# Time-mixing stage: pa as one tile of two banks, D in X's bank, Y's state products beside X's, groups issued in a fixed order

## The chip, the cores and the metric

The kernel runs on one core of a Trainium2 chip. The metric is the device time of one execution in microseconds (us), the median of the runs. In the profile PE is the matmul engine and PEld its weight loads, DVE the vector engine, ACT the scalar engine, POOL the general engine, and SP issues the transfers (DMA).

## The reference

Two layers over 1024 latent and 256 context tokens of width 1024. Each layer norms its input, projects it, runs three mixers side by side and merges them. The change lies in the first mixer, a recurrence over tokens in two directions, with 8 heads of 64 x 64 state:

```python
def rwkv7_scan(r, v, kk, decay, k_dir, akk, state0, reverse):
    """S_t = S_{t-1} (diag(w_t) - kk_t^T (a_t kk_t)) + v_t^T k_t ;  y_t = S_t r_t."""
    def step(s, inp):
        r_t, v_t, kk_t, w_t, k_t, akk_t = inp
        s_kk = jnp.einsum('bhvk,bhk->bhv', s, kk_t)
        s = s * w_t[:, :, None, :] - s_kk[..., None] * akk_t[:, :, None, :] + v_t[..., None] * k_t[:, :, None, :]
        return s, jnp.einsum('bhvk,bhk->bhv', s, r_t)
    s_fin, ys = lax.scan(step, state0, xs, reverse=reverse)
```

The context's recurrence runs first and hands its last state to the latent tokens. In the last layer only the latent tokens' y is used. Everything is float32.

## The kernel before

**The stage.** `rwkv_stage` works through 20 chunks of 64 tokens, both directions d and all heads at once. Heads come as 4 pairs `pr`; `p` is the member of a pair, and it says which half of the 128 partitions its operands lie in (0 to 63 or 64 to 127). So a group of products over d, pr and p is 16 calls, and each call on fp32 operands is two matmul instructions in the profile, 32 in all. The transposes (L617) are one each.

**prep(c)**, which runs ahead, loads bkT, kr and uv (L588, L589, L594), multiplies them into pa (L604), masks pa on DVE into mb (L607), copies mb's diagonal blocks to dg on ACT (L612), transposes bkT on PE into pt (L617) and copies that to bk on ACT (L618). Then DVE transposes dg to at (L624) and inverts small triangular blocks step by step (P and R, L640 to L657); their inverse is tt (L659). bkT, dg, at, R and P have one buffer each, bk two, mb and kr three.

**chain(c)** carries the state S. X gathers products of mb and uv (L667) and of kr and S (L670). Twice, ACT copies X to x1 (L675), PE multiplies by tt into U (L679), and DVE (p = 0) and ACT (p = 1) copy U to uv (L684); between the two, X gets one more product (L689). D is the product of bk and uv (L693), from which DVE makes the next S (L696, L697). Y, where the chunk has an output (all 20 chunks in layer 0, 16 in layer 1), gathers S with kr (L703) and uv with mb (L706); ACT copies it to yst (L709, L710).

**PSUM.** It has 8 banks. The pool `pre` has two slots of one bank, used in turn for pa of p = 0, pa of p = 1 and pt; `chn` has a bank each for X, U, D and Y; `pj`, outside the stage, has two for projections.

**Order.** The program is written chunk after chunk, but a scheduler sets the order of instructions on each engine when the kernel is built: whatever is ready first by its own reckoning goes first, and earlier code has priority. Each engine then runs its instructions in that order, and so does SP its transfers. Between the stage's products the scheduler places projections that don't depend on it (pjt, L150: `z_stage`, at the end `g_stage`), three matmuls of up to 512 columns for each block of weights. `tc.issue_after(ins)` makes what is traced in its block stand behind `ins` on that engine; it asks for the order alone, not for a wait.

Of the kernel before, what the change touches and what calls it, by code (L numbers as in the profile page):

```python
# [8 lines left out]
F32 = mybir.dt.float32  # L9
# [3 lines left out]
ALU = mybir.AluOpType  # L13
AX = mybir.AxisListType
PSUM = bass.MemoryType.PSUM
# [22 lines left out]
def tile_backbone(ctx: ExitStack, tc: tile.TileContext, xT_in, cond_in, w_mod, vecs, w_in, d_up, a_up,  # L38
                  qkg, lqk, w_br, w_out, consts, rope, out):
    nc = tc.nc  # L40
    te, ve, se, gp, dma = nc.tensor, nc.vector, nc.scalar, nc.gpsimd, nc.sync

    def pool(name, bufs=1, space=None, es=ctx):
        kw = {} if space is None else {"space": space}
        return es.enter_context(tc.tile_pool(name=name, bufs=bufs, **kw))
# [19 lines left out]
    mask = cst[:, C_MASK:C_MASK + 128]  # L65
# [68 lines left out]
    def run_late(ins=None):  # L134
        due = []
        for e in late[:]:
            e[0] -= 1
            if ins is None or e[0] <= 0:
                due.append(e[1])
                late.remove(e)  # L140
        for f in due:
            with tc.issue_after(ins) if ins is not None else ExitStack():
                f()

    def mm3(ps, terms):
        n = 3 * len(terms)
# [426 lines left out]
    def rwkv_stage(l):  # L573
        full = l < NL - 1
        es = ExitStack()
        rp = pool("rp", es=es)
        pre = pool("pre", bufs=2, space=PSUM, es=es)
        chn = pool("chn", bufs=1, space=PSUM, es=es)
        units = [(d, pr, p) for d in range(2) for pr in range(4) for p in range(2)]
        f8 = lambda a: a.rearrange("p d a v -> p (d a) v")  # L580

        def prep(c):
# [11 lines left out]
                    dma.dma_start(out=uv[64 * p:64 * p + 64, d, p].rearrange("t a v -> t (a v)"),  # L594
                                  in_=v_dr[l][d][row:row + 64, 256 * p:256 * p + 256])
            mb = rp.tile([128, 2, 2, 4, 128], F32, tag="mb", name="mb", bufs=3)
            mk = mask[:, 0:ny].unsqueeze(1).to_broadcast([128, 4, ny])
            for d in range(2):

                pas = [pre.tile([128, 4, 128], F32, tag="pre", name="pa") for p in range(2)]  # L600
                for pr in range(4):
                    for p in range(2):
                        s = slice(64 * p, 64 * p + 64)
                        te.matmul(out=pas[p][:, pr, 0:ny], lhsT=bkT[s, 4 * d + pr, :], rhs=kr[s, 4 * d + pr, 0:ny],  # L604
                                  start=True, stop=True)
                for p in range(2):
                    ve.tensor_tensor(out=mb[:, d, p, :, 0:ny], in0=pas[p][:, :, 0:ny], in1=mk, op=ALU.mult)  # L607
            dg = rp.tile([128, 2, 4, 32], F32, tag="dg", name="dg", bufs=1)
            for p in range(2):
                for q in range(2):  # L610
# [1 line left out]
                    se.copy(out=dg[s], in_=mb[s, :, p, :, 32 * q:32 * q + 32])  # L612
            bk = rp.tile([128, 2, 4, 128], F32, tag="bk", name="bk", bufs=2)
            for d in range(2):
                pt = pre.tile([128, 4, 128], F32, tag="pre", name="pt")
                for pr in range(4):
                    te.transpose(out=pt[:, pr, :], in_=bkT[:, 4 * d + pr, :], identity=ident)  # L617
                se.copy(out=bk[:, d], in_=pt)  # L618
# [42 lines left out]

        def chain(c, st, S, yst):
            y, kr, mb, bk, uv, tt = st
            half = [slice(64 * p, 64 * p + 64) for p in range(2)]
            X = chn.tile([128, 2, 4, 64], F32, tag="X", name="X")
            for d, pr, p in units:
                te.matmul(out=X[half[1 - p], d, pr, :], lhsT=mb[half[p], d, p, pr, 0:64], rhs=uv[half[p], d, p, pr, :],  # L667
                          start=(d == 0 and pr == 0), stop=False, skip_group_check=True)
            for d, pr, p in units:
                te.matmul(out=X[half[1 - p], d, pr, :], lhsT=kr[half[p], 4 * d + pr, 0:64], rhs=S[half[p], d, pr, :],  # L670
                          start=False, stop=False, skip_group_check=True)
            U = chn.tile([128, 2, 4, 64], F32, tag="U", name="U")
            for q in range(2):
                x1 = rp.tile([128, 2, 4, 64], F32, tag="xs", name="xs", bufs=1)
                se.copy(out=x1, in_=X)  # L675
                for d, pr, p in units:
                    b0 = 64 * (1 - p)
                    s = slice(b0 + 32 * q, b0 + 32 * q + 32)
                    te.matmul(out=U[s, d, pr, :], lhsT=tt[s, 4 * d + pr, :], rhs=x1[s, d, pr, :], start=True,  # L679
                              stop=True, skip_group_check=True)  # L680
                for p, cp in ((0, ve.tensor_copy), (1, se.copy)):
                    b0 = 64 * (1 - p)
                    s = slice(b0 + 32 * q, b0 + 32 * q + 32)
                    cp(out=uv[s, :, p], in_=U[s])  # L684
                if q == 0:
                    for d, pr, p in units:
                        b0 = 64 * (1 - p)
                        s = slice(b0, b0 + 32)
                        te.matmul(out=X[b0 + 32:b0 + 64, d, pr, :], lhsT=mb[s, d, p, pr, 32:64],  # L689
                                  rhs=uv[s, d, p, pr, :], start=False, stop=True, skip_group_check=True)  # L690
            D = chn.tile([128, 2, 4, 64], F32, tag="D", name="D")
            for d, pr, p in units:
                te.matmul(out=D[half[p], d, pr, :], lhsT=bk[:, d, pr, half[p]], rhs=uv[:, d, p, pr, :],  # L693
                          start=True, stop=True, skip_group_check=True)
            Sn = rp.tile([128, 2, 4, 64], F32, tag="S", name="S", bufs=2)
            ve.tensor_tensor(out=Sn, in0=D, in1=S, op=ALU.add)  # L696
            ve.tensor_tensor(out=f8(Sn), in0=f8(Sn), in1=dd_all[0][:, c, :].unsqueeze(2).to_broadcast([128, 8, 64]),  # L697
                             op=ALU.mult)
            if y:
                Y = chn.tile([128, 2, 4, 64], F32, tag="Y", name="Y")  # L700

                for d, pr, p in units:
                    te.matmul(out=Y[half[p], d, pr, :], lhsT=S[half[p], d, pr, :], rhs=kr[half[p], 4 * d + pr, 64:128],  # L703
                              start=(d == 0 and pr == 0), stop=False, skip_group_check=True)
                for d, pr, p in units:
                    te.matmul(out=Y[half[p], d, pr, :], lhsT=uv[:, d, p, pr, :], rhs=mb[:, d, p, pr, 64:128],  # L706
                              start=False, stop=True, skip_group_check=True)
                i = c % 2
                se.copy(out=yst[:, 0, :, 64 * i:64 * i + 64], in_=Y[:, 0])  # L709
                se.copy(out=yst[:, 1, :, 64 - 64 * i:128 - 64 * i][:, :, ::-1], in_=Y[:, 1])  # L710
                if i:
                    w = c // 2
                    for d, tb in enumerate((1024 + 128 * w if w < 2 else 128 * w - 256, 1152 - 128 * w)):
                        dma.dma_start(out=yd_dr[l][d][:, :, tb:tb + 128], in_=yst[:, d])
            return Sn
# [458 lines left out]
```

## Time and profile before

| | |
|---|---|
| median of 3 runs | 3865.43 us (3864.11 to 3884.64) |
| the profiled execution | 3869.96 us |
| its span, first to last instruction | 3868.2 us |
| mean granted clock of PE | 0.974 of full speed |
| time mixing, layer 0 | about 740 to 1270 us |
| time mixing, layer 1 | about 2690 to 3205 us |
| instructions | 71042 |

A row of a group of instructions names the line of the kernel, the engine, the operation, the tile written and the tiles read, the shapes (partitions x elements), how many there are, their busy time, the mean time of one and the idle time before them with what ended it. A row of the timeline begins with the start in us from the span's start and the time from the first start to the last end of the instructions that it merges. Matmuls overlap, so a merged row of n takes less than n times one.

### The profile page before, as it was taken

Reading aid. Unit: us, or ns where it says so; the run is one execution under the profiler, and the core shown is the slowest. Engines: PE = TensorE matmul, PEld = TensorE weight load, DVE = VectorE, ACT = ScalarE, POOL = GpSimd, SP = SyncE. Lnnn points to the kernel's source line nnn. Section 1 sums busy time; section 2 is a strip of 40 time slices with the busy share of each in tenths; the row PEclk is TensorE's granted clock in tenths of the full one; section 3 lists DMA queues with packets and bytes.
Section 4 is the critical chain, followed back from the end, with each engine's and each line's share of the span. In section 5 each row is a group of like instructions: output and inputs, shape, how many; then the busy total and the mean of one; then the engine's idle time right before and its main releaser. Section 6 shows DMA issues by size and latency. Waiting matters only on the chain.

```text
span 3868.2 us, 71042 instructions
## 1 busy us (share of the span) xinstructions
PE 3702.9 (96%) x28540; PEld 3040.2 (79%) x28540; DVE 2525.7 (65%) x5248; ACT 1629.4 (42%) x3055; POOL 87.2 (2%) x252
## 2 busy tenths in 40 slices
PE   8999999999999999998999999999999999999999
PEld 5778988877777888886776778988877768888667
DVE  6746732488887677735655765634888876777572
ACT  5654211222222667644434763212322326676540
POOL 0100000000000000000000110000000000000000
PEclk8999999999998999999999999999999999999999
DMA  5545232332222322226764455222232214222573
GB/s 201 145 127 147 74 108 96 115 93 88 93 82 67 105 82 83 79 81 224 223 202 129 120 155 141 93 88 88 83 102 91 92 59 116 84 92 77 201 251 125
DMA packets 378570, 454.74 MB, mean 118 GB/s; under 512 B 119808, under 2 KB 266752, under 8 KB 378240
## 3 DMA queue, kind: packets, MB, share of 16 engines
q1 hardware_dynamic: 376320, 447.58, 37.1%
q8 instruction: 224, 3.67, 0.4%
q0 software_dynamic: 1920, 2.62, 0.3%
q14 instruction: 106, 0.87, 0.1%
HBM read 300.66 MB, written 146.80 MB: 116 GB/s over the span
## 4 chain that ended last, share of the span: by engine, by line
PE 52%; DVE 18%; ACT 4%; DMA 4%; issue 3%; SPq 1%; DVEq 0%; POOL 0%; ACTq 0%; POOLq 0%
PE pjt L150 34%; DVE P L648 4%; PE s L815 4%; PE o L150 3%; DVE R L652 2%; PE U L679 2%; PE at L841 2%; PE pa L604 2%; PE X L689 1%; DVE P L654 1%; DVE mb L607 1%; DVE R L657 1%; PE pt L617 1%; DVE uv L684 1%; DVE wlo L114 1%
## 5 line engine op out<-in xcount | busy, mean ns | idle before, releaser
L150 PE MATMUL pjt<-hT0h,whi 128*128 128x512 f32 x1488 | 558.7, 376 | 3.6 <-ACT hT0h L282 1.4
L150 PE MATMUL pjt<-hT0l,whi 128*128 128x512 f32 x1488 | 546.6, 367 | 1.1 <-DVE hT0l L283 0.9
L150 PE MATMUL pjt<-hT0h,wlo 128*128 128x512 f32 x1488 | 544.8, 367 | 0.1
L150 PE MATMUL pjt<-hT1h,whi 128*128 128x512 f32 (+1 forms) x1072 | 429.4, 401 | 4.5 <-ACT tl L317 1.9
L150 PE MATMUL pjt<-hT1l,whi 128*128 128x512 f32 (+1 forms) x1072 | 425.4, 397 | 0.0
L150 PE MATMUL pjt<-hT1h,wlo 128*128 128x512 f32 (+1 forms) x1072 | 423.6, 395 | 1.3 <-DVE wlo L114 1.3
L113 ACT CAST whi<-wraw 128x1024 fp32r<-128x1024 f32 x208 | 217.9, 1049 | 372.2 <-PE pjt L150 344.8
L114 DVE TENSOR_TENSOR wlo<-wraw,whi 128x1024 fp32r<-128x1024 f32 x208 | 255.1, 1227 | 153.9 <-ACT whi L113 148.3
L150 PEld LDWEIGHTS pjt<-hT0h,whi 128*128 128x128 f32 x1488 | 288.0, 194 | 54.9 <-issue 10.6
L150 PEld LDWEIGHTS pjt<-hT0l,whi 128*128 128x128 f32 x1488 | 288.4, 194 | 47.2 <-issue 5.7
L150 PEld LDWEIGHTS pjt<-hT0h,wlo 128*128 128x128 f32 x1488 | 288.1, 194 | 44.2 <-issue 2.4
L826 ACT ACTIVATE p<-s,mx 128x512 f32<-128x512 f32 (+1 forms) x400 | 240.2, 611 | 87.7 <-DVE mx L821 85.6
L817 DVE TENSOR_REDUCE mx<-s 128x1 f32<-128x512 f32 (+1 forms) x400 | 228.8, 588 | 71.7 <-PE s L815 70.7
L150 PEld LDWEIGHTS pjt<-hT1h,whi 128*128 128x128 f32 x1072 | 205.3, 192 | 53.0 <-issue 8.1
L150 PEld LDWEIGHTS pjt<-hT1h,wlo 128*128 128x128 f32 x1072 | 205.7, 192 | 43.6 <-DVE wlo L114 2.5
L150 PEld LDWEIGHTS pjt<-hT1l,whi 128*128 128x128 f32 x1072 | 205.1, 191 | 43.9 <-issue 5.6
L648 DVE TENSOR_TENSOR P<-at,R 128x16 f32<-128x16 f32 (+6 forms) x280 | 215.3, 769 | 8.7
L604 PE MATMUL pa<-kr,bkT 64*128 64x128 f32 (+1 forms) x1280 | 154.8, 301 | 49.5 <-DVE mb L607 46.8
L604 PEld LDWEIGHTS pa<-kr,bkT 64*128 64x128 f32 x1280 | 128.9, 194 | 74.5 <-DVE mb L607 61.8
L815 PE MATMUL s<-kh,qs 128*128 128x512 f32 (+1 forms) x400 | 146.2, 372 | 5.5 <-issue 2.8
L150 PE MATMUL pjt<-ya,whi 128*128 128x512 f32 (+1 forms) x448 | 136.9, 390 | 6.8 <-ACT ya L113 5.7
L815 PE MATMUL s<-kl,qs 128*128 128x512 f32 (+1 forms) x400 | 142.4, 362 | 0.0
(268 smaller groups left out, 8022.8 us busy)
## 6 DMA issues: line engine op xcount, KB each, us to landing
wraw<-in_w_in_dram SPq DMA_DIRECT2D x148, 512.0 KB, 4.2
kr<-kr SPq DMA_DIRECT2D x68, 512.0 KB, 3.3
wm<-in_w_mod_dram SPq DMA_DIRECT2D x48, 512.0 KB, 3.8
th<-fth SPq DMA_DIRECT2D x96, 256.0 KB, 2.0
bkT<-bk SPq DMA_DIRECT2D x40, 512.0 KB, 3.4
wraw<-in_w_br_dram SPq DMA_DIRECT2D x36, 512.0 KB, 4.5
th<-th SPq DMA_DIRECT2D x64, 256.0 KB, 3.8
wraw<-in_w_out_dram SPq DMA_DIRECT2D x24, 512.0 KB, 4.0
```

Source lines behind the costliest of these rows:

```text
L113: se.copy(out=hi, in_=src)
L114: ve.tensor_tensor(out=lo, in0=src, in1=hi, op=ALU.subtract)
L150: i = te.matmul(out=ps, lhsT=a, rhs=b, start=(c == 0), stop=(c == n - 1))
L604: te.matmul(out=pas[p][:, pr, 0:ny], lhsT=bkT[s, 4 * d + pr, :], rhs=kr[s, 4 * d + pr, 0:ny], start=True, stop=True)
L607: ve.tensor_tensor(out=mb[:, d, p, :, 0:ny], in0=pas[p][:, :, 0:ny], in1=mk, op=ALU.mult)
L648: ve.tensor_tensor(out=pv, in0=at[:, i1:32, i0:i1].rearrange("p j i -> p i j").unsqueeze(2) .to_broadcast([128, 4, nm, n]), in1=R[:, i1:32 ...
L652: ve.tensor_reduce(out=R[:, i0:i1, b + 1:8], in_=pv, axis=AX.X, op=ALU.add)
L679: te.matmul(out=U[s, d, pr, :], lhsT=tt[s, 4 * d + pr, :], rhs=x1[s, d, pr, :], start=True, stop=True, skip_group_check=True)
L815: te.matmul(out=s[:, :n], lhsT=qs[:, c, 128 * e:128 * e + 128], rhs=kd[c][x][:, c0:c0 + n], start=(x == 0), stop=(x == 1))
L817: ve.tensor_reduce(out=mx[:, x0:x0 + 1], in_=s[:, :n], axis=AX.X, op=ALU.max)
L826: se.activation(out=p[:, o:o + n], in_=tiles[x0][:, :n], func=AF.Exp, scale=0.125, bias=mx[:, 3:4], accum_out=sums[:, x0:x0 + 1])
L841: te.transpose(out=pt[:, k, :], in_=ex[0][:, 128 * (k0 + k):128 * (k0 + k) + 128], identity=ident)
```

## The change

pa becomes one tile of two banks, one for each p, in a pool with a slot for pa and a slot for pt; one DVE instruction masks both halves. D uses the slot of X (tag XD), so that X, D share a bank, and Y and U keep theirs. The products of S for Y are issued in turn with those for X, in one list: a product for X, written to the half 1 - p, then one for Y with the same S, written to the half p. Y's second products stand behind D's. All groups go through `run_mm`, which makes each product stand behind the one before it; other work may still come between. The order of the halves is (1, 0) for the chain's groups and (0, 1) for pa.

```diff
+    def run_mm(calls):
+
+        with ExitStack() as order:
+            for out, lhsT, rhs, start, stop in calls:
+                i = te.matmul(out=out, lhsT=lhsT, rhs=rhs, start=start, stop=stop, skip_group_check=True)
+                order.close()
+                order.enter_context(tc.issue_after(i.ins))
...
-        pre = pool("pre", bufs=2, space=PSUM, es=es)
+        pre = pool("pre", bufs=1, space=PSUM, es=es)
         chn = pool("chn", bufs=1, space=PSUM, es=es)
-        units = [(d, pr, p) for d in range(2) for pr in range(4) for p in range(2)]
+
+        units = [(d, pr, p) for d in range(2) for pr in range(4) for p in (1, 0)]
+        half = [slice(64 * p, 64 * p + 64) for p in range(2)]
...
-                pas = [pre.tile([128, 4, 128], F32, tag="pre", name="pa") for p in range(2)]
-                for pr in range(4):
-                    for p in range(2):
-                        s = slice(64 * p, 64 * p + 64)
-                        te.matmul(out=pas[p][:, pr, 0:ny], lhsT=bkT[s, 4 * d + pr, :], rhs=kr[s, 4 * d + pr, 0:ny],
-                                  start=True, stop=True)
-                for p in range(2):
-                    ve.tensor_tensor(out=mb[:, d, p, :, 0:ny], in0=pas[p][:, :, 0:ny], in1=mk, op=ALU.mult)
+                pa = pre.tile([128, 2, 4, 128], F32, tag="pa", name="pa")
+                run_mm([(pa[:, p, pr, 0:ny], bkT[half[p], 4 * d + pr, :], kr[half[p], 4 * d + pr, 0:ny], True, True)
+                        for pr in range(4) for p in range(2)])
+                ve.tensor_tensor(out=mb[:, d].rearrange("q p a t -> q (p a) t")[:, :, 0:ny],
+                                 in0=pa.rearrange("q p a t -> q (p a) t")[:, :, 0:ny], in1=mk, op=ALU.mult)
...
-                pt = pre.tile([128, 4, 128], F32, tag="pre", name="pt")
+                pt = pre.tile([128, 4, 128], F32, tag="pt", name="pt")
...
+            X = chn.tile([128, 2, 4, 64], F32, tag="XD", name="X")
+            Y = chn.tile([128, 2, 4, 64], F32, tag="Y", name="Y") if y else None
+            first = lambda d, pr: d == 0 and pr == 0
+            calls = [(X[half[1 - p], d, pr, :], mb[half[p], d, p, pr, 0:64], uv[half[p], d, p, pr, :], first(d, pr), False)
+                     for d, pr, p in units]
             for d, pr, p in units:
...
+                kc, sv = kr[half[p], 4 * d + pr, :], S[half[p], d, pr, :]
+                calls.append((X[half[1 - p], d, pr, :], kc[:, 0:64], sv, False, False))
+                if y:
+
+                    calls.append((Y[half[p], d, pr, :], sv, kc[:, 64:128], first(d, pr), False))
+            run_mm(calls)
...
+            D = chn.tile([128, 2, 4, 64], F32, tag="XD", name="D")
+            calls = [(D[half[p], d, pr, :], bk[:, d, pr, half[p]], uv[:, d, p, pr, :], True, True) for d, pr, p in units]
+            if y:
+                calls += [(Y[half[p], d, pr, :], uv[:, d, p, pr, :], mb[:, d, p, pr, 64:128], False, True)
+                          for d, pr, p in units]
+            run_mm(calls)
```

The groups of U (L679) and of X's later products (L689) are passed to `run_mm` in the same way.

## Rows read from the trace of the kernel before

**Rows 1.** The page's first part: busy time, share of the span and instructions of an engine.
```profile
PE 3702.9 (96%) x28540; PEld 3040.2 (79%) x28540; DVE 2525.7 (65%) x5248; ACT 1629.4 (42%) x3055; POOL 87.2 (2%) x252
```

**Rows 2.** Busy time of each engine in three stretches, time mixing of layer 0, of layer 1, and a stretch of layer 0's attention: start and end, length, then busy us (instructions) of PE, PEld, DVE, ACT, POOL, the granted clock, the DMA share and GB/s.
```profile
740.00:1270.00 530.00, 494.51 (x6859) 407.85 (x6860) 438.16 (x982) 149.56 (x308) 6.86 (x38) 0.93 0.29 88
2690.00:3205.00 515.00, 482.46 (x6501) 393.11 (x6500) 430.96 (x960) 148.13 (x294) 6.86 (x38) 0.94 0.28 87
1300.00:1690.00 390.00, 388.59 (x2300) 329.73 (x2299) 279.11 (x687) 271.06 (x640) 0.00 (x0) 1.00 0.24 76
```

**Rows 3.** The chain of waits by line, in the stretch 740 to 1270 us and in 2690 to 3205 us (shares of the stretch).
```profile
by line: PE pjt L150 27.0%; DVE P L648 14.0%; PE U L679 7.7%; DVE R L652 7.5%; PE pa L604 6.7%; PE X L689 4.9%; DVE P L654 4.1%; PE pt L617 3.9%; DVE mb L607 3.8%; DVE R L657 3.6%; DVE S L696 2.4%; issue 2.4%; DVE uv L684 2.3%; DVE S L697 2
...
by line: PE pjt L150 25.1%; DVE P L648 14.8%; DVE R L652 8.5%; PE U L679 7.4%; PE pa L604 5.6%; PE X L689 5.1%; DVE P L654 4.2%; DVE mb L607 3.9%; DVE R L657 3.6%; PE pt L617 3.2%; DVE uv L684 2.9%; DVE S L696 2.5%; issue 2.5%; DVE S L697 2
```

**Rows 4.** Waits of PE and of DVE, each in the stretch of layer 0 and then in that of layer 1: who waited for whom, us in total, times, the longest.
```profile
PE pa L604 <- DVE mb L607: 25.5, 19, 1.7
...
PE pa L604 <- DVE mb L607: 21.3, 17, 1.7
...
DVE uv L684 <- PE U L679: 34.2, 26, 6.0
...
DVE uv L684 <- PE U L679: 38.9, 24, 8.3
```

**Rows 5.** pa: its group over the whole run, two of its bursts in the timeline, and the number of its matmuls that run in two short stretches (start and end, length, busy us, number, granted clock, DMA).
```profile
L604 PE MATMUL pa<-kr,bkT 64*128 64x128 f32 (+1 forms) x1280 | 154.8, 301 | 49.5 <-DVE mb L607 46.8
...
904.70 0.72 PE L604 MATMUL pa<-kr,bkT 64*128 64x128 f32 x8
...
933.49 2.01 PE L604 MATMUL pa<-kr,bkT 64*128 64x128 f32 x16 [1.36 <-DVE mb L607]
...
904.69:904.72 0.03, 0.02 (x2) 1.00 1.05 273
...
933.52:933.60 0.08, 0.08 (x1) 1.00 0.12 51
```

**Rows 6.** DVE's product mb over the whole run, the nearest DVE product of 1024 elements, and one mb with the DVE instruction that follows it in the timeline.
```profile
L607 DVE TENSOR_TENSOR mb<-pa,cst 128x512 f32<-128x512 f32 (+1 forms) x160 | 104.6, 655 | 21.7 <-PE pa L604 21.6
...
L114 DVE TENSOR_TENSOR wlo<-wraw,whi 128x1024 fp32r<-128x1024 f32 x208 | 255.1, 1227 | 153.9 <-ACT whi L113 148.3
...
909.25 0.68 DVE L607 TENSOR_TENSOR mb<-pa,cst 128x512 f32<-128x512 f32 x1
...
909.84 0.34 DVE L654 TENSOR_TENSOR P<-t,R 128x112 f32<-128x112 f32 x1
```

**Rows 7.** The state products of X and Y of one chunk, timeline of PE.
```profile
902.86 0.97 PE L670 MATMUL X<-S,kr 64*64 64x64 f32 x26
...
903.73 0.22 PE L703 MATMUL Y<-kr,S 64*64 64x64 f32 x1
903.73 0.22 PE L670 MATMUL X<-S,kr 64*64 64x64 f32 x1
...
903.79 0.98 PE L703 MATMUL Y<-kr,S 64*64 64x64 f32 x27
```

**Rows 8.** The same chunk from the copy of X to its later products, timeline.
```profile
904.11 0.59 ACT L675 COPY xs<-X 128x512 f32<-128x512 f32 x1 [1.39 <-PE X L670]
...
916.40 0.67 DVE L659 STREAM_TRANSPOSE tt<-R 128x256 f32<-128x256 f32 x1
...
917.18 0.95 PEld L679 LDWEIGHTS U<-xs,tt 32*32 32x32 f32 x32 [0.45 <-ACT dg L612]
...
919.43 0.29 PE L689 MATMUL X<-uv,mb 32*32 32x64 f32 x2
...
920.54 1.08 PE L689 MATMUL X<-uv,mb 32*32 32x64 f32 x30
```

**Rows 9.** The new state and the copy of Y at the end of two chunks, and the first state product of the next, timeline.
```profile
902.07 0.69 DVE L697 TENSOR_TENSOR S<-S,dd 128x512 f32<-128x512 f32 x1
902.32 0.40 ACT L710 COPY yst<-Y 128x256 f32<-128x256 f32 x1
...
927.69 0.68 DVE L697 TENSOR_TENSOR S<-S,dd 128x512 f32<-128x512 f32 x1
927.78 0.40 ACT L710 COPY yst<-Y 128x256 f32<-128x256 f32 x1
```

**Rows 10.** The reload of bkT on SP's queue, the copies of dg and of bk on ACT, and the transpose that reads dg, timeline.
```profile
913.99 0.33 SPq L588 DMA_DIRECT2D bkT<-bk  x1
...
915.31 1.65 ACT L612 COPY dg<-mb 32x256 f32<-32x256 f32 x4 [1.76 <-DVE at L624]
...
926.56 1.07 ACT L618 COPY bk<-pt 128x512 f32<-128x512 f32 x2 [1.60 <-PE D L693]
...
937.53 1.25 DVE L624 STREAM_TRANSPOSE at<-dg 128x1024 f32<-128x1024 f32 x1
```

**Rows 11.** Busy time of the engines in two short stretches, columns as in rows 2 (the granted clock is the third number from the end).
```profile
933.50:935.40 1.90, 1.90 (x16) 1.80 (x16) 1.87 (x4) 0.00 (x0) 0.00 (x0) 1.00 0.03 11
936.10:939.20 3.10, 3.10 (x14) 2.80 (x14) 3.10 (x7) 0.38 (x1) 0.03 (x1) 0.50 0.00 0
```

More of the change, by code (lines that the diff above doesn't have):

```diff
@@ L596, in prep @@
             mb = rp.tile([128, 2, 2, 4, 128], F32, tag="mb", name="mb", bufs=3)
-            mk = mask[:, 0:ny].unsqueeze(1).to_broadcast([128, 4, ny])
+            mk = mask[:, 0:ny].unsqueeze(1).to_broadcast([128, 8, ny])
             for d in range(2):
-                pas = [pre.tile([128, 4, 128], F32, tag="pre", name="pa") for p in range(2)]
-                for pr in range(4):
-                    for p in range(2):
-                        s = slice(64 * p, 64 * p + 64)
-                        te.matmul(out=pas[p][:, pr, 0:ny], lhsT=bkT[s, 4 * d + pr, :], rhs=kr[s, 4 * d + pr, 0:ny],
-                                  start=True, stop=True)
-                for p in range(2):
-                    ve.tensor_tensor(out=mb[:, d, p, :, 0:ny], in0=pas[p][:, :, 0:ny], in1=mk, op=ALU.mult)
+                pa = pre.tile([128, 2, 4, 128], F32, tag="pa", name="pa")
[3 more added lines that the diff above has]
+                                 in0=pa.rearrange("q p a t -> q (p a) t")[:, :, 0:ny], in1=mk, op=ALU.mult)
             dg = rp.tile([128, 2, 4, 32], F32, tag="dg", name="dg", bufs=1)
@@ L663, in chain @@
             y, kr, mb, bk, uv, tt = st
-            half = [slice(64 * p, 64 * p + 64) for p in range(2)]
-            X = chn.tile([128, 2, 4, 64], F32, tag="X", name="X")
-            for d, pr, p in units:
[L667 to L671, printed above, removed]
+            X = chn.tile([128, 2, 4, 64], F32, tag="XD", name="X")
[3 more added lines that the diff above has]
+                     for d, pr, p in units]
+            for d, pr, p in units:
+                kc, sv = kr[half[p], 4 * d + pr, :], S[half[p], d, pr, :]
[3 more added lines that the diff above has]
+            run_mm(calls)
             U = chn.tile([128, 2, 4, 64], F32, tag="U", name="U")
@@ L675, in chain @@
                 se.copy(out=x1, in_=X)
[L676 to L680, printed above, removed]
+                part = [slice(64 * (1 - p) + 32 * q, 64 * (1 - p) + 32 * q + 32) for p in range(2)]
+                run_mm([(U[part[p], d, pr, :], tt[part[p], 4 * d + pr, :], x1[part[p], d, pr, :], True, True)
+                        for d, pr, p in units])
                 for p, cp in ((0, ve.tensor_copy), (1, se.copy)):
-                    b0 = 64 * (1 - p)
-                    s = slice(b0 + 32 * q, b0 + 32 * q + 32)
-                    cp(out=uv[s, :, p], in_=U[s])
+                    cp(out=uv[part[p], :, p], in_=U[part[p]])
                 if q == 0:
[L686 to L694, printed above, removed]
+                    run_mm([(X[64 * (1 - p) + 32:64 * (1 - p) + 64, d, pr, :], mb[part[p], d, p, pr, 32:64],
+                             uv[part[p], d, p, pr, :], False, True) for d, pr, p in units])
+            D = chn.tile([128, 2, 4, 64], F32, tag="XD", name="D")
[4 more added lines that the diff above has]
+            run_mm(calls)
             Sn = rp.tile([128, 2, 4, 64], F32, tag="S", name="S", bufs=2)
@@ L699, in chain @@
             if y:
[L700 to L707, printed above, removed]
                 i = c % 2
```

## The prediction

> **What bounds the kernel now.** I read the page's busy shares first, then the stretches of the two time-mixing stages, then the chain of waits inside them, then the waits, and last the timeline of two chunks. Over the whole run PE is busy 96%, DVE 65% [rows 1]. That average hides the stage: in the two stretches of time mixing, 1045 us together, PE is busy 977 us (93.5%) and DVE 869 us (83%), where in layer 0's attention PE has no gap at all [rows 2]. So this stage has two nearly full engines, each with its own fixed order, and the reader should see which holds the other. The chain of waits says: both. In layer 0 its PE lines are pjt 27.0%, U 7.7%, pa 6.7%, X (L689) 4.9% and pt 3.9%; its DVE lines P, R and mb make 33% [rows 3]. The waits go both ways as well: PE stands 25.5 and 21.3 us for mb before a pa group, DVE stands 34.2 and 38.9 us for U [rows 4]. A microsecond taken from PE alone is therefore worth something, but less than a microsecond.
>
> **pa, the PE side.** Of the two orders that pa takes in the trace, one is slow. The 16 matmul instructions of a group at 933.49 us take 2.01 us, one running at a time when they begin; the 8 at 904.70 take 0.72 us, and two are running within the first 0.03 us [rows 5]. Each fp32 product is two instructions (1280 for 640 calls). In the code neighbours of a pair read the two halves of the partitions and write two tiles; I take the fast group to be the one in which the halves alternate, the slow one that in which the scheduler put one tile's products first because its slot was free earlier. The change forces alternation. A single one lasts 0.30 us, so neighbours are (0.72 - 0.30)/7 = 0.06 us apart and 16 take 0.72 + 8 x 0.06 = 1.20 us. On average a group of 16 now costs 154.8/80 = 1.94 us. Saved: 0.74 x 80 = 59 us of PE.
>
> **X and Y.** At 902.86 the state products of X and Y take until 903.79 + 0.98 = 904.77, 1.91 us for 64 instructions, mostly one tile after the other at (0.97 - 0.22)/25 = 0.03 us each. For a moment the two mix, and there an X, two Y's and their partners start within 0.06 us, four in the time of two [rows 7]. If all 64 do so: 16 x 0.06 + 0.22 = 1.18 us; saved 0.73 x 36 chunks that have a Y = 26 us. The other end of this price is 0: the chip may not keep up four tiles. I take 26, since the mixed rows are these very instructions.
> One rule speaks against it. Here both partition halves write X's one bank, in its two output halves, and the rows give 0.03 us a matmul, not the (2.01 - 0.30)/15 = 0.11 of pa's slow group [rows 5, 7]. The Trainium skill (TensorEngine Tiling (Array Packing), Gotcha 1: PSUM Pressure) says that different row tiles can't use the same PSUM bank at once. By that rule, taken without regard to partitions, the mixing would save nothing and the sum below would end 11 us later, at 3835, still a part of the forecast; I give it one chance in ten there, since the rows are this kernel's own.
>
> **Splits.** With the halves taken in the order (0, 1), two instructions of X (L689) go out alone at 919.43, 0.29 us, then projection work, and the other 30 only at 920.54 [rows 8]. The first half's values come from DVE, the second's from ACT, later. With (1, 0) the first product waits for the later copy and the pair stays in the group. Two in a stream cost 2 x (1.08 - 0.22)/29 = 0.06, so about 0.22 us x 40 = 9 us of PE.
>
> **mb.** 160 DVE products of 512 become 80 of 1024. Now 104.6 us; the nearest row of 1024 elements, wlo, takes 1227 ns, so 80 x 1.227 = 98 us, 6 saved. From start to start two small ones take 0.59 us each (909.25 to 909.84) [rows 6]; with the same overlap of 0.09 a large one takes 1.14, and 80 x 0.04 = 3 us are saved. A few chunks have half the width, which makes it at most 10. I take 6. The ACT and DMA instructions stay the same in number.
>
> **Moved at no cost.** (1) D lies in X's bank: the next chunk's first X products (L667) now start only when DVE has read D (L696), and as one ordered list the state products stand behind them. The 32 of L667, at 0.03 each, make that about 1 us later for X. Its cover is large: x1 of the chunk is copied at 904.11, and U, which needs it, starts at 917.18 because tt is finished only at 916.40 + 0.67 [rows 8]. Without that cover it would cost 1 us x 40. (2) pt has its own bank and no longer waits for mb, but its second tile now waits for ACT's copy of the first, which waits for D of an earlier chunk: bkT's reload, at 913.99 now, then comes after the copy at 926.56 [rows 10]. The reload stands in SP's queue, so kr, uv and the projections' stores behind it are late too; pa is late next, then mb and dg. The cover: dg copied at 915.31 is used by the transpose at 937.53, 20 us later [rows 10]. If it were gone, the 12.6 us of delay would fall on every chunk, but then the scheduler's whole order would differ. (3) One slot for pa: its second group waits for one mb of 1.2 us instead of two halves. PE waits there already [rows 4]; I count no change, with the ends at the present 47 us, gained or lost.
>
> **The sum.** PE saves 59 + 26 + 9 = 94 us. How much reaches the end? pa itself lies on the chain of waits for 6.7% of 530 and 5.6% of 515, 64 us of its 154.8, or 41% [rows 3, 5]. With that share 94 gives 39 us. mb: 3.8% and 3.9%, 40 us of 104.6, so 6 gives 2. Together 41. The profiled execution took 3870.0 us (its span 3868.2 and 1.8 around it), so 3829; the median of the runs, 3865.4, is 4.6 below it, so **3824 us**, 1.1% faster.
>
> **The rivals.** A difference below 0.5%, 19 us, can't be told from none in this kernel.
> - *DVE holds the stage.* DVE has 869 us of work; its wait for U is at the end of a run copy, product, copy, product that PE's savings hardly touch. Then PE only waits longer for mb, and the time is that of mb's saving: 3865 - 6 = 3859. For it: 47 us of PE already spent in that wait. Against it: the projection pieces on the chain.
> - *PE holds it wholly.* All 94 + 6 arrive: 3765. Against it: PE would be left with 883 us of work and DVE has 863, so that neither could stand while the other works, and the waits are mutual.
> - *The clock.* At 936.10 to 939.20 the granted clock is 0.50, that is 1.2 GHz; just before it PE had waited 1.36 us for mb and then run the slow pa group at 1.00 [rows 5, 11]. The stages' means are 0.93 and 0.94 [rows 2], so 0.07 x 530 + 0.06 x 515 = 68 us of full-speed work are lost now. Shorter groups and longer waits could make such stretches twice as many: 68 x 0.41 = 28 back, 3852. None at all would give 3796. The Trainium skill (TensorE: Matmul & The Clock Gate, HAM oscillation — how this bites in real kernels) states that idle gaps of the engine bring the half rate; by it the first of these two is the likelier.
> - *Slower: Y's bank holds up X.* The ordered list puts a Y product after each X product, so X's second waits until ACT has copied the previous Y out. Now that copy ends at 902.72 and S is ready at 902.76; the next time at 928.18 and 928.37 [rows 9]: a margin of 0.04 to 0.2 us. If ACT does bk's copies (1.07) and dg's (1.65) first, PE stands 2.7 us with all its projection work behind it, 97 us over 36 chunks: 3824 + 97 = 3921. It decides from (41 + 19)/36 = 1.7 us a chunk. Against it: only X's chain has 12 us to spare, and the bk copies were ahead of Y's at 926.56 already.
>
> **Chances.** Forecast (3800 to 3846) 0.50; DVE holds 0.15; clock 0.09; PE wholly 0.10; slower 0.16. Faster by over 0.5%: 0.50 + 0.10 = 0.60; within: 0.24; slower: 0.16. The range leaves out the last part of PE wholly and most of the slower case: 3775 to 3885.
>
> **What would show it.** pa's busy time near 80 x 1.20 = 96 us; the 64 X and Y instructions in about 1.2 us; no X pair alone before its group; 80 mb of about 1.2 us; both stages together some 40 us shorter, attention unchanged. I am wrong if DVE's busy share in the stage goes up to 90% or more and pa's wait for mb grows by what pa saves; if the clock of the stages falls below 0.9; if X or Y shows a wait for yst; or if more projection work is placed in the stage, so that the gain shows up in attention instead.

## The result, and the profile after

The changed kernel takes 3904.84 us against 3868.03 for the kernel before, runs of both on the same chip: a ratio of 1.0087, interval [1.0067, 1.0107]. It is slower by 0.9%, on the other side of the forecast. The profiled execution took 3887.5 us, the shortest of the twelve, at a mean granted clock of 0.958; the longest took 3922.2 at 0.950. The page's first line and the three stretches, which answer to [rows 1, 2]:

```profile
PE 3649.2 (94%) x28540; PEld 3002.1 (77%) x28540; DVE 2526.9 (65%) x5168; ACT 1635.0 (42%) x3055; POOL 84.1 (2%) x252
```

```profile
740.00:1270.00 530.00, 459.60 (x6837) 382.96 (x6837) 438.04 (x941) 152.17 (x307) 6.88 (x38) 0.87 0.27 87
2690.00:3205.00 515.00, 448.65 (x6384) 370.38 (x6384) 429.63 (x925) 146.80 (x286) 6.88 (x38) 0.87 0.26 84
1300.00:1690.00 390.00, 388.12 (x2298) 329.33 (x2297) 278.35 (x684) 270.22 (x636) 0.00 (x0) 1.00 0.25 76
```

PE works 54 us less over the run and is still late: in the stage it stands more, and its clock is 0.87 instead of 0.93 and 0.94; attention is as it was. To measure the stage by itself I take, in each kernel and layer, the time from the first S (the product with D) to the last one, 20 chunks. Stretches cut there, kernel before and then after:

```profile
779.50:1257.80 478.30, 446.05 (x6292) 364.60 (x6289) 404.87 (x899) 136.20 (x280) 6.50 (x36) 0.93 0.27 85
2717.90:3192.30 474.40, 442.91 (x6112) 358.17 (x6112) 402.98 (x890) 135.90 (x270) 6.50 (x36) 0.94 0.27 86
```

```profile
777.20:1257.10 479.90, 414.28 (x6293) 342.01 (x6291) 405.16 (x862) 138.19 (x278) 6.52 (x36) 0.87 0.26 85
2720.80:3211.20 490.40, 426.31 (x6121) 348.85 (x6121) 403.59 (x855) 138.48 (x269) 6.52 (x36) 0.86 0.26 84
```

The stage of both layers together goes from 952.7 to 970.3 us, 17.6 more, and the span from 3868.2 to 3885.7, 17.5 more: of these two executions, all of it lies here. It is half of the 36.8 us between the medians. PE's busy time falls by 48 us (889.0 to 840.6), its idle time rises by 66 (63.7 to 129.7). Work that the half clock took, length times (1 - clock) of each layer, goes from 62 to 131 us; it is called lost work below. The groups of pa and of mb, which answer to [rows 5, 6], and U:

```profile
L149 PE MATMUL pa<-kr,bkT 64*128 64x128 f32 (+1 forms) x1280 | 131.1, 340 | 96.7 <-DMA bkT<-bk 72.2 <-DVE mb L613 24.4
L149 PE MATMUL U<-xs,tt 32*32 32x64 f32 x2560 | 106.9, 243 | 33.2 <-DVE P L647 24.7 <-DVE tt L666 7.9
L613 DVE TENSOR_TENSOR mb<-pa,cst 128x1024 f32<-128x1024 f32 (+1 forms) x80 | 92.7, 1159 | 33.4 <-PE pa L149 32.6
```

The waits of PE and the largest of DVE, layer 0 and then layer 1, against [rows 4]:

```profile
PE pa L149 <- DMA bkT<-bk: 40.3, 18, 3.2
PE U L149 <- DVE P L647: 12.2, 10, 4.0
PE pa L149 <- DVE mb L613: 11.2, 7, 3.1
...
DVE uv L691 <- PE U L149: 37.3, 27, 4.3
...
PE pa L149 <- DMA bkT<-bk: 31.9, 17, 2.8
PE pa L149 <- DVE mb L613: 13.1, 8, 2.9
...
DVE uv L691 <- PE U L149: 50.0, 27, 6.5
```

bkT, which was no wait before, is now the largest; DVE's wait for U has grown from 73 to 87 us. One chunk of layer 1 in the timeline, and the clock in the last of it:

```profile
2902.54 0.53 SPq L598 DMA_DIRECT2D bkT<-bk  x1
...
2906.39 1.16 PE L149 MATMUL pa<-kr,bkT 64*128 64x128 f32 x16 [1.60 <-DMA bkT<-bk]
2906.59 1.64 DVE L655 TENSOR_TENSOR P<-at,R 128x784 f32<-128x784 f32 x1
...
2909.15 1.23 DVE L631 STREAM_TRANSPOSE at<-dg 128x1024 f32<-128x1024 f32 x1
...
2910.88 1.22 DVE L613 TENSOR_TENSOR mb<-pa,cst 128x1024 f32<-128x1024 f32 x1
...
2912.15 0.69 PE L149 MATMUL pa<-kr,bkT 64*128 64x128 f32 x2 [2.85 <-DVE mb L613]
2912.78 1.92 PE L149 MATMUL U<-xs,tt 32*32 32x64 f32 x32
2914.63 2.07 PE L149 MATMUL pa<-kr,bkT 64*128 64x128 f32 x14
```

```profile
2914.00:2918.00 4.00, 4.00 (x54) 3.60 (x51) 2.98 (x7) 0.58 (x1) 0.00 (x0) 0.50 0.18 66
```

The first pa group takes 1.16 us, as forecast. It is ready at 2907.55, but its mb stands in DVE's fixed order behind P, R and at and starts at 2910.88. With one slot the second group can only follow mb. PE stands 2.85 us, the clock goes to 0.50, and U takes 1.92 us instead of 1.08 and the rest of pa 2.07.

### The profile page after: what moved, and what is told of

It is laid out like the page before. It is cut to its first block, busy times and chain, and to the rows that moved or that the text cites. A ratio compares the mean times of both kernels' runs of the same rounds, so it can differ in the third digit from the quotient of the medians.

```text
span 3885.7 us, 70975 instructions
## 1 busy us (share of the span) xinstructions
PE 3649.2 (94%) x28540; PEld 3002.1 (77%) x28540; DVE 2526.9 (65%) x5168; ACT 1635.0 (42%) x3055; POOL 84.1 (2%) x252
## 5 line engine op out<-in xcount | busy, mean ns | idle before, releaser
L149 PE MATMUL pa<-kr,bkT 64*128 64x128 f32 (+1 forms) x1280 | 131.1, 340 | 96.7 <-DMA bkT<-bk 72.2
L149 PEld LDWEIGHTS pa<-kr,bkT 64*128 64x128 f32 x1280 | 106.7, 230 | 126.9 <-DMA bkT<-bk 53.0
```

The lines of the kernel that those rows point to most:

```text
L149: i = te.matmul(out=out, lhsT=lhsT, rhs=rhs, start=start, stop=stop, skip_group_check=True)
```

## The experiments

All numbers of the stage are those of the view above: length of both layers, PE busy, the clock of layer 0 and layer 1, and lost work of both. They are of the one profiled execution, which can lie off the median: e6 3854.3 us (median 3845.8), e12 3849.5 (3840.2), e13 3930.2 (3953.7).

| run | what it is | ratio to before, interval | stage us | PE busy us | clock | lost us |
|---|---|---|---|---|---|---|
| before | | 1 | 952.7 | 889.0 | 0.93, 0.94 | 62 |
| after | the change | 1.0087 [1.0067, 1.0107] | 970.3 | 840.6 | 0.87, 0.86 | 131 |
| e1 | change, pt in pa's slot | 1.0113 [1.0084, 1.0142] | 981.7 | 853.2 | 0.86, 0.86 | 137 |
| e2 | change, pt doesn't read bkT | 1.0172 [1.0149, 1.0196] | 1004.9 | 856.8 | 0.81, 0.86 | 166 |
| e3 | chain's part alone | 1.0131 [1.0110, 1.0152] | 1000.6 | 866.8 | 0.86, 0.89 | 125 |
| e4 | prep's part and D in X's bank | 1.0215 [1.0170, 1.0259] | 1037.2 | 921.2 | 0.84, 0.87 | 151 |
| e6 | pa's order alone | 0.9941 [0.9922, 0.9960] | 934.8 | 868.0 | 0.93, 0.96 | 52 |
| e7 | D in X's bank alone | 1.0190 [1.0160, 1.0221] | 1018.4 | 933.2 | 0.85, 0.91 | 123 |
| e8 | e3, D in its own bank | 1.0029 [1.0012, 1.0046] | 957.0 | 852.3 | 0.90, 0.92 | 86 |
| e9 | e3 with unread matmuls | 1.0470 [1.0433, 1.0507] | 1012.3 | 894.8 | 0.81, 0.82 | 187 |
| e10 | X's products behind D, by order | 1.0167 [1.0141, 1.0193] | 1011.5 | 922.4 | 0.86, 0.90 | 122 |
| e11 | e1, D in its own bank | 1.0114 [1.0087, 1.0140] | 997.2 | 869.3 | 0.85, 0.87 | 140 |
| e12 | chain's part, D own, two slots, pa's order | 0.9922 [0.9897, 0.9947] | 929.8 | 824.2 | 0.91, 0.94 | 70 |
| e13 | prep's part alone, pt in pa's slot | 1.0214 [1.0160, 1.0269] | 1007.4 | 901.5 | 0.90, 0.88 | 111 |

**Is it bkT's late reload?** e1 lets pt take pa's slot as one tile, so that the transposes don't wait for ACT; e2 lets them read a constant, so that bk isn't the transpose of bkT.

```diff
-                pt = pre.tile([128, 4, 128], F32, tag="pt", name="pt")
+            pt = pre.tile([128, 2, 4, 128], F32, tag="pa", name="pt")
...
-                se.copy(out=bk[:, d], in_=pt)
+                se.copy(out=bk[:, d], in_=pt[:, d])
```

> The changed kernel, but pt is one tile of both directions in pa's slot, so that bkT is free again when the transposes are done and its reload no longer stands behind the copy to bk, which waits for D. Theory A (the late reload of bkT holds PE at pa, 72 us of waits, and its idle time lowers the clock): the wait for bkT falls below 10 us, the stages' granted clock goes from 0.87 back to about 0.93, and the time to 3825 to 3860. Theory B (pa's single slot makes PE wait for mb): pt waits for mb as well now, so the time stays at 3890 or more and the waits of PE for mb grow. Theory C (X's list behind D and Y): the time stays at 3890 or more with the waits for bkT gone.

```diff
-                    te.transpose(out=pt[:, pr, :], in_=bkT[:, 4 * d + pr, :], identity=ident)
+                    te.transpose(out=pt[:, pr, :], in_=ident, identity=ident)
```

> The changed kernel, but the transposes into pt read a constant instead of bkT (bk then holds the wrong numbers; the work is the same). pt, its slot, its copy and their waits are as in the changed kernel; only bkT is released by pa alone. Theory A: the wait for bkT falls below 10 us and the time to 3825 to 3860. Theories B and C: at 3890 or more, with pa's wait for mb (24 us of PE) and U's late start still there.

The wait for bkT goes down from 72 to 34 us in both, not below 10, and neither is faster. In e1 PE stands 35 us more at pa for which the profile names no releaser, so e1 says little. In e2 PE stands for what DVE brings, layer 0 and layer 1:

```profile
PE U L149 <- DVE P L647: 28.0, 16, 4.5
PE pa L149 <- DVE mb L613: 23.1, 13, 3.5
PE pa L149 <- DMA bkT<-bk: 22.0, 9, 3.5
...
PE U L149 <- DVE P L647: 26.0, 15, 3.6
PE pa L149 <- DVE mb L613: 17.3, 11, 3.2
PE pa L149 <- DMA bkT<-bk: 12.3, 5, 2.8
```

The largest row of the waits shows where PE stood; taken away by half, it went to the next rows. That the reload costs nothing isn't shown, but it isn't needed for a loss: e3, next, has nearly no wait for bkT and loses more than the change.

**Which half of the change?** e3 keeps the chain's part (D in X's bank, the list of X and Y, the halves in the order (1, 0)) with pa and pt as before; e4 the reverse, but for D, which stays in X's bank.

```diff
-        pre = pool("pre", bufs=1, space=PSUM, es=es)
+        pre = pool("pre", bufs=2, space=PSUM, es=es)
...
-                pa = pre.tile([128, 2, 4, 128], F32, tag="pa", name="pa")
+                pas = [pre.tile([128, 4, 128], F32, tag="pre", name="pa") for p in range(2)]
```

> The chain of the changed kernel (D in X's bank, Y's products beside X's, fixed order) with the prep of the kernel before: pa as two tiles, two slots shared with pt, two mb per direction. Theory A: bkT is released as before, so no loss; PE saves 26 + 9 us, some 14 at the end, 3850. Theory B: the same, 3850. Theory C: as slow as the change, about 3900.

> The prep of the changed kernel (pa as one tile in one slot, fixed order, one mb per direction, pt in its own slot) with the chain's groups as in the kernel before, except that D shares X's bank so that the banks suffice. Theory A: the wait of PE for bkT is there with 50 us or more and the time is at least that of the change, 3900. Theory B: also about 3900, with most of the waits at mb. Theory C: about 3840.

Both halves lose (3917.4 and 3956.8 us), and more than the whole. So they don't add, and single parts were run.

**pa's order, against the kernel before.**

```diff
+                run_mm([(pas[p][:, pr, 0:ny], bkT[64 * p:64 * p + 64, 4 * d + pr, :],
+                         kr[64 * p:64 * p + 64, 4 * d + pr, 0:ny], True, True) for pr in range(4) for p in range(2)])
```

> The kernel before with one edit: pa's products issued in the fixed order that alternates the halves; two tiles and two slots as before. Theory D (PE's saved time turns into waiting at pa for mb, the granted clock falls to half in the wait, and the projections that stand ahead of U in PE's order then run at half rate): pa's busy time falls from 155 to about 100 us, PE's wait for mb and the time at the half clock grow, and the time is 3865 to 3900. Theory E (sharing X's bank with D is what costs): the edit is clean, 3845.

22 us faster, what the prediction's pa term times its share gives (59 x 0.41 = 24). pa's own busy time is 144.1 us though, only 11 below [rows 5], and lost work falls by 10 as well (62 to 52): the agreement in size is luck. That PE's savings always come back as waiting fell with this run.

**D in X's bank, against the kernel before; and the new chain without it.**

```diff
-            X = chn.tile([128, 2, 4, 64], F32, tag="X", name="X")
+            X = chn.tile([128, 2, 4, 64], F32, tag="XD", name="X")
...
-            D = chn.tile([128, 2, 4, 64], F32, tag="D", name="D")
+            D = chn.tile([128, 2, 4, 64], F32, tag="XD", name="D")
```

> The kernel before with one edit: D takes X's bank. Theory D: no saving, so nothing to lose, 3855 to 3885. Theory E: 3900 to 3920.

> As e3_chain_only (the chain of the change with the prep of before), but D has a bank of its own. Theory D: as slow as e3_chain_only, 3900 to 3925. Theory E: 3850.

e8 is e3 with D's tag taken back. The tag alone costs 75 us, beyond what theory E gave it, and taking it out of the chain's part brings 39 back, so that e8 (3878.7) lies between both theories. In e8 PE's busy time in the stage is 37 us below the kernel before, and none of it reaches the end: PE's idle time rises by 41 (63.7 to 104.7). PE waits 72 us for mb before pa instead of 47, and 22 for S instead of 6. The 37 are near the forecast for X, Y and the splits (26 + 9) by chance: D and Y's second products fell by 29 more (rows under Splits, below), and pa rose by 15, to 169.7.

**Bank or place in the order?** e10 leaves D its bank and only puts X's first products (L667) behind D of the chunk before.

```diff
+            with tc.issue_after(last_d[0]) if last_d[0] is not None else ExitStack():
+                for d, pr, p in units:
+                    te.matmul(out=X[half[1 - p], d, pr, :], lhsT=mb[half[p], d, p, pr, 0:64], rhs=uv[half[p], d, p, pr, :],
+                              start=(d == 0 and pr == 0), stop=False, skip_group_check=True)
```

> The kernel before, D in its own bank, with one edit: X's first products (mb and uv) are put behind the D group of the chunk before in PE's order, by order alone, with no wait. Theory F (the shared bank costs because these 32 instructions leave the gap between U and D, where PE waits for the copies of U, and so all of PE's order shifts): as slow as e7_xd_only, 3915 to 3945. Theory G (the shared bank costs by its wait: X stands until DVE has read D): no loss, 3860 to 3880.

It costs 66 us with no bank shared, so the order alone is enough. First the kernel before, where these 32 instructions run between U and D, while ACT and DVE copy U; the first two of D and of Y go out alone:

```profile
922.45 1.08 PE L679 MATMUL U<-xs,tt 32*32 32x64 f32 x32
923.46 1.03 PE L667 MATMUL X<-uv,mb 64*64 64x64 f32 x28
923.65 0.70 DVE L684 COPY uv<-U 32x512 f32<-32x512 f32 x1 [1.39 <-PE U L679]
...
924.42 0.33 PE L693 MATMUL D<-uv,bk 128*64 128x64 f32 x2
...
924.59 0.28 PE L706 MATMUL Y<-mb,uv 128*64 128x64 f32 x2
```

Then e10, later in a chunk, and its clock there:

```profile
890.96 1.16 PE L604 MATMUL pa<-kr,bkT 64*128 64x128 f32 x16
...
894.23 1.60 DVE L648 TENSOR_TENSOR P<-at,R 128x784 f32<-128x784 f32 x1
895.74 0.69 DVE L607 TENSOR_TENSOR mb<-pa,cst 128x512 f32<-128x512 f32 x1
...
896.48 2.07 PE L604 MATMUL pa<-kr,bkT 64*128 64x128 f32 x8 [3.00 <-DVE mb L607]
...
900.03 0.63 DVE L659 STREAM_TRANSPOSE tt<-R 128x256 f32<-128x256 f32 x1
...
903.74 0.69 DVE L607 TENSOR_TENSOR mb<-pa,cst 128x512 f32<-128x512 f32 x1 [2.99 <-PE pa L604]
904.00 1.08 PE L682 MATMUL U<-xs,tt 32*32 32x64 f32 x32
```

```profile
896.00:899.00 3.00, 2.52 (x10) 2.30 (x11) 3.00 (x6) 0.00 (x0) 0.17 (x1) 0.50 0.00 0
```

Here PE stands 3.00 us for an mb that DVE does behind its largest P, runs pa and a line of projections at half clock, and comes to U at 904.00, though tt is there at 900.66. Then DVE stands 2.99 us for pa. In the kernel before U starts 0.11 us after tt [rows 8]. These are two single chunks; over all 40 chunks a chunk's first U starts 0.8 us after its tt on average in the kernel before, 1.8 in e10 and 1.9 in e7. Over the whole run of e10:

```profile
L604 PE MATMUL pa<-kr,bkT 64*128 64x128 f32 (+1 forms) x1280 | 162.0, 311 | 83.4 <-DVE mb L607 80.9 <-DMA uv<-v 2.4
L696 PE MATMUL D<-uv,bk 128*64 128x64 f32 x1280 | 62.0, 234 | 0.1
```

Before D, in the place that the 32 instructions left, PE doesn't stand (0.1 us): other work fills it. It stands at pa, 80.9 us for mb instead of 46.8. That this other work is what is missing at pa fits the rows and isn't shown by itself. Lost work rises by 60 us in e10 and by 61 in e7, about as much as their stages (59 and 66).

**Holding the clock up.** e9 is e3 with 12 matmuls of 512 columns, which nobody reads, between the two pa groups.

```diff
+                if d == 0:
+                    wt = chn.tile([128, 512], F32, tag="W", name="wt")
+                    wk = hT[0][0][0]
+                    with tc.issue_after(lastpa.ins):
+                        for _ in range(12):
+                            wl = te.matmul(out=wt, lhsT=wk[:, 0, 0:128], rhs=wk[:, 0, :], start=True, stop=True)
```

> As e3_chain_only, with 12 matmuls of 512 columns that nobody reads, into a bank of their own, put between the two pa groups of a chunk, where PE stands still for mb: 12 x 0.23 us x 40 = 110 us of added work on PE. Theory D: they keep the granted clock up (half-clock time of the stages from 256 us to below 150) and fill a wait, so the kernel is faster than e3_chain_only in spite of them: 3870 to 3900. Theory E, or if the wait itself is the loss and the clock is not: 3917 or more, up to 4020.

It takes 4050.7 us, beyond both theories. The scheduler moved other work away for the added matmuls: 1071 of projections are left in the stage, where e3 has 1572. The clock of the stages fell further, to 0.81 and 0.82, so the run says nothing on what a steady clock would give.

**Single slot, and the version without both losses.** e11 is e1 with D's tag taken back. e13 is the kernel before with pa as one tile of two banks in one slot, one mb, and pt in the same slot (in the change pt has a slot of its own, for which no bank is left here). e12 has the new chain with D in its own bank, and pa as two tiles in two slots in the fixed order.

> As e1_pt_in_pa (the whole change, with pt in pa's slot), but D has a bank of its own, which pt's bank gives. Theory E (sharing X's bank is what costs): 40 to 65 us faster than e1_pt_in_pa, 3840 to 3867, so at least as fast as the kernel before. Without it: 3900 to 3915.

> The kernel before with the prep of the change alone (pa one tile in one slot, fixed order, one mb per direction; pt as one tile in the same slot) and D in its own bank. By the prediction's terms for pa and mb: 3868 - 24 - 2 = 3842. If the single slot makes PE wait more for mb: 3855 to 3890.

> As e8_chain_d_own (chain of the change, D in its own bank, two pa tiles), with pa's products in the fixed order as in e6_pa_order. If the parts add up: 3879 - 22 = 3857. If the chain's new order hides pa's saving: 3875 to 3885.

The one slot, with pt in it, costs 83 us by itself (e13), beyond what was expected, and stays when D has its bank: e11 (3913.2) is 73 us slower than e12 (3840.2), which differs from it in the slots of pa and pt and in mb alone. Either of the two moved things is enough to lose. The way of the loss is another than in e10: U starts 0.15 us after tt on average in e13 and 0.2 in the change, so nothing on PE holds it up once tt is there; it waits for tt. With neither, e12 beats the kernel before by 0.8%, 17 us more than the sum of its parts gave; e6 alone has 0.6%, and their intervals overlap.

**Through the projections, or the stage's own chain?** In e14 to e17 the projections and attention stand on PE behind the stage's last D, so the stage runs alone: the kernel before, e10, e13 and the change. Their totals are 1.09 to 1.10 of the kernel before, since that work is no longer hidden.

```diff
+        with tc.issue_after(end_d[0]):
+            for b in range(2):
+                if b not in VDE[l]:
+                    vd_block(l, b, lambda: sp.tile([128, 512], F32, tag="fth", name="fvd", bufs=FTH))
+            z_stage(l, sp)
+            attn_stage(l)
+            g_stage(l, sp)
```

> The kernel before, but all projection work of the layer that can run beside the stage (the z projections, the late vd blocks, what attention and g ask of PE) stands on PE behind the stage's last D, so that PE has only the stage's own work in it. The total grows by what is no longer hidden, some 150 to 300 us by the projections that stand in the stages now (pjt 27% and 25% of the two stretches); what is read is the length of the stages, first state S to last S, both layers together: 953 us in the kernel before. Theory 'projections' (the changed order costs time because projections placed in PE's fixed order delay pa and U): with none there the stage is shorter, 800 to 900 us. Theory 'chain alone' (the stage's own chain sets the length): 930 to 955 us.

> The same setting, with X's first products behind D of the chunk before, by order alone (with projections in the stage this order took the stages from 953 to 1011 us, 58 more). Theory 'projections': within 10 us of the stages of the kernel without projections in the stage and the old order, or up to 15 us more, since without projections the 32 products only move inside PE's idle time. Theory 'chain alone': again 40 to 60 us more.

> The same setting, with pa as one tile of two banks in one slot that it shares with pt, and one mb (with projections in the stage: 1007 against 953 us). Theory 'projections': within 15 us of the old layout without projections. Theory 'chain alone' (one slot makes pa's second group, mb, pt and dg stand one behind the other, so the stage's own chain is longer): 40 to 60 us more.

> The same setting, with the whole change (with projections in the stage: 970 against 953 us). Theory 'projections': equal to the old layout without projections or 10 to 40 us shorter, since PE's saving of some 94 us then meets nothing that gives it back. Theory 'chain alone': 15 to 40 us longer than the old layout without projections.

The stage of e14 and then of e17 in the same view:

```profile
784.90:1269.60 484.70, 367.07 (x5517) 318.70 (x5514) 376.34 (x862) 109.58 (x236) 6.52 (x36) 0.63 0.18 56
2904.60:3389.00 484.40, 358.76 (x5297) 310.97 (x5299) 375.01 (x860) 107.28 (x228) 6.51 (x36) 0.64 0.17 54
```

```profile
782.50:1255.80 473.30, 321.59 (x5554) 281.68 (x5554) 377.74 (x826) 111.65 (x236) 6.48 (x36) 0.65 0.19 58
2889.80:3357.60 467.80, 315.84 (x5330) 276.72 (x5332) 376.09 (x826) 109.11 (x228) 6.46 (x36) 0.64 0.18 57
```

| both layers, us | with projections | alone |
|---|---|---|
| kernel before | 952.7 | 969.1 (e14) |
| X's products behind D | 1011.5, +59 | 982.0 (e15), +13 |
| one slot | 1007.4, +55 | 992.4 (e16), +23 |
| the change | 970.3, +18 | 941.1 (e17), -28 |

Three quarters of the first loss and over half of the second are gone when no projection lies in between, at a clock of 0.63 to 0.65 in all four runs, and the change is faster: e17's whole run takes 4210.1 us, e14's 4243.4. e16 is 8 us beyond what the first theory allowed, so a part of the slot's price is the chain's own. e14 itself missed both expectations: with all projections gone the stage is not shorter, and the total grew by 376 us, not by 150 to 300.

## Why the prediction was wrong

- **pa, 59 us: the size right, the clock left out.** A group takes 1.16 us where 1.20 was worked out, but the row's busy time falls by 24 us only, to 131.1. The mean of one instruction went from 301 to 340 ns, since more groups run at half clock, as the 14 at 2914.63 do.
- **X and Y, 26 us: right.** In the timeline of after two X and two Y go out every 0.06 us:

```profile
2900.49 0.23 PE L149 MATMUL X<-S,kr 64*64 64x64 f32 x2
...
2900.50 0.26 PE L149 MATMUL Y<-kr,S 64*64 64x64 f32 x2
...
2900.55 0.22 PE L149 MATMUL X<-S,kr 64*64 64x64 f32 x2
```

  All 64 lie between 2899.92 and 2901.12, 1.2 us. The rule of the Trainium skill that was weighed against this (TensorEngine Tiling (Array Packing), Gotcha 1: PSUM Pressure) took nothing away here.
- **Splits, 9 us: too small.** Only X's pair was counted. D and Y's second products had the same split (924.42 and 924.59 above), and the fixed order closed it. Layer 0's stretch, kernel before and after:

```profile
L693 PE MATMUL D<-uv,bk 128*64 128x64 f32 x640 | 30.4, 231 | 0.0
L706 PE MATMUL Y<-mb,uv 128*64 128x64 f32 x640 | 30.2, 225 | 0.0
...
L149 PE MATMUL D<-uv,bk 128*64 128x64 f32 x640 | 23.0, 225 | 0.0
L149 PE MATMUL Y<-mb,uv 128*64 128x64 f32 x640 | 22.1, 222 | 0.0
```

  Over the run they fall by 29 us (60.9 to 46.5 and 54.3 to 39.7), a term that the prediction put at nothing.
- **mb, 6 us: it saved 12** (104.6 to 92.7), still small.
- **The share of 41%** was the step that joined PE's savings to the end. It has no fixed value: 37 us gave nothing in e8. In the stage alone PE's busy time falls by 88 us from e14 to e17 and the stage by 28, 32%, but both moved things are in that too, so the nearness is luck.
- **Moved at no cost (1) failed.** The prediction asked when X's data were needed and found 12 us of cover until tt. It didn't ask what else moves when they leave their place between U and D. Moved out of it, they cost 66 us by order alone (e10) and 75 by the bank (e7); the standing shows at pa, and lost work grows by 60.
- **Moved at no cost (2)** named the right next victim, pa, and judged 20 us of cover enough; PE stood 72 us for bkT. But e2, with half of that wait, wasn't faster, and e3, nearly without it, lost too.
- **Moved at no cost (3) failed.** "PE waits there already" was counted as no change, with ends at 47 us. One slot, with pt in it, costs 83 us net of the part's own savings (e13). The wait that it was priced by didn't grow: PE stands for mb before pa 47 us before, 24 after and 32 in e13. What grew is the wait of U for DVE's P and tt (9 us before, 33 after, 27 in e13), the wait for bkT (72 after, 20 in e13) and lost work (62, 131, 111). One way to it is the chunk above, in which mb stands behind P, R and at and PE with one slot can't go on; that it is the way over the whole run isn't shown.
- **The rivals.** The clock was the right one and priced far too low: it was given 28 us back and a time of 3852. Its condition, twice as many such stretches, came true: in the prediction's own stretches lost work went from 68 to 136 us. What failed is that 0.41 of it would be the price. The prediction's bound, stages below 0.9, came true as well. The Trainium skill (TensorE: Matmul & The Clock Gate, HAM oscillation — how this bites in real kernels) has idle gaps bring the half rate; the rows at 896.48 and 2912.15 agree, with waits of 3.00 and 2.85 us ahead of 0.50. DVE did not become fuller (84.4 and 82.3% of the two stages, 84.6 and 84.9% before), and Y's bank held nothing up: no wait for yst stands among PE's.

The sum of the stage, by rows: the forecast took 94 us from PE; 48 came off its busy time, and 66 were added to its idle time: +18. By the clock's records in the traces PE was busy at half clock for 126 us before and for 253 after. Half of the 127 more, 63 us, is what the half clock took back, so at full clock some 112 us would have come off. By this estimate PE's saving was there, with the D and Y terms beside the forecast ones, and the clock took more than half of it.

**What stays open.** Whether the order costs through its places or through the half clock. Projections ahead of U can be the way in e7 and e10, not in the change, where U starts 0.2 us after tt. For the clock more speaks. Executions of one program, which all have one order, differ with their clock: the kernel before took 3856.8 us at 0.978 and 3880.1 at 0.972 (runs beside e6), e6 3829.2 at 0.987 and 3854.3 at 0.977, the change 3887.5 at 0.958 and 3922.2 at 0.950. That is 25 to 43 us for 0.01; by this estimate the fall from 0.975 before to 0.955 after (medians) is worth 50 to 87 us, more than the 37 that were lost. And lost work grows by what the stage grows in e7 and e10, and nearly so in e13 (49 and 55). It isn't shown as the cause: why the clock differs between executions isn't on record, and longer waits come with a lower clock. In e14 to e17 it had nowhere to fall, so that the losses shrink there fits both, and e9 didn't hold it up. Each edit also made the scheduler order the stage anew, so a run's loss is that of the order it got; e7 and e10, which reach the same place by two ways, agree within 9 us.

## What to carry to other kernels

Before calling a moved group free, ask what else moves into the place that it leaves, and where that is missing then: 32 instructions, 1 us of work a chunk, cost 66 us by their place alone. Before taking a PSUM slot away, look at when its reader comes in the other engine's fixed order, not only at the reader's 1.2 us. Where waits and half clock already alternate, don't scale lost work by the share that held for busy time. And undo one part at a time: here the order of pa alone was worth 0.6%, and the rest of the change hid it.

## What was not expected of the hardware

- Taking all projections out of the stage (e14) left it 16 us longer: its own products then run at a clock of 0.63, and U's row goes from 89.2 to 153.3 us.
- A wait of 2.85 us was paid twice: 0.50 followed, and the next groups took nearly double the time (U 1.92 us against 1.08, 14 instructions of pa 2.07 against 1.16 for 16).
- Twelve matmuls more per chunk did not raise the clock: e9 had 0.81 and 0.82, e3 without them 0.86 and 0.89. 501 matmuls of projections left the stage in e9, so that it holds 12344 in all, e3 12440.
- One program varies with its clock: ten executions of e6 run from 3829.2 us at 0.987 to 3854.3 at 0.977, with no other difference on record.
